# A hybrid decoder layer: bulk loads of the branch stage on ACT's queue, RG-LRU gate matmuls farther behind their split, one gate pair moved behind the RG-LRU pairs

## The chip, the cores and the metric

The kernel runs on one core of one Trainium2 chip. The metric is device microseconds of one execution. Engines are named as in the profile: PE is TensorE (PEld its weight loads), DVE is VectorE, ACT is ScalarE, POOL is GpSimd, SP is SyncE, which here does nothing but issue DMAs. "SPq", "ACTq" and "POOLq" are the instruction streams in which those engines issue DMAs. TensorE's granted clock is written as a share of 2.4 GHz; 0.5 would be its lower level, 1.2 GHz.

## The reference, cut to what matters

One layer of a decoder on 1104 tokens (16 meta, 1024 prompt, 8 x 8 decode), model width 1024. All arithmetic is float32 in the reference.

```
xn = rms_norm(x);  u, gate_a, q, f, i, og, m_a, m_b = split(xn @ w_in)     # eight blocks of 1024 columns
uc = causal_conv(u)
r, ig = sigmoid(block_diag(uc, rg_w)), sigmoid(block_diag(uc, ig_w))       # 8 blocks of 128 x 128
a = exp(-8 r softplus(-lam));  h = scan(a, sqrt(1 - a^2) * ig * uc)        # RG-LRU
y_a = h * gelu(gate_a)
y_b = rms_norm(hgrn2(q, f, i)) * silu(og)                                  # HGRN2
mixed = sigmoid(m_a) * (y_a @ w_branch_a) + sigmoid(m_b) * (y_b @ w_branch_b)
x = x + rms_norm(mixed @ w_out);  x = x + rms_norm(squared_relu_mlp(rms_norm(x)))
```

## The kernel before, in words

Every large matmul is done in float16 with three products (high x high, high x low, low x high), so weights and activations are split into a high half (ACT, a scaled copy) and a low half (DVE, the remainder); for weights this is `w_split`, lines 194 and 196. A *pair* is two 128-column blocks of a weight matrix against one activation matrix, computed for two halves of the tokens. Most pairs use a Strassen form: 7 products per half, each product 12 matmuls (lines 359, 361, 362 in `prod`), in the order S3, S1, A11, S2, A22, S4, A12 over four PSUM banks. Because A22 adds into the bank of S3, ACT has to copy that bank out (line 372) before the fifth product can start; bank by bank the same holds for the next ones. Pairs named in `NOSTR` use the plain form (`upair`): 8 products per half, and only 4 weight splits in place of 7.

Weights come in ahead of use, one pair ahead. SP loads a 512 KB `ws` tile (`raw_dma`, L164) and a 256 KB `sa` tile (`sum_load`, L182), later one more block (L239, or L261 in the plain form). For the Strassen form POOL adds further blocks onto these tiles with accumulating DMAs (L184, L233, L236, L242); the plain form has none of these four.

The stretch that matters runs from the pairs of `LSEQ` to the last branch pair:

1. **`LSEQ`**: eight RG-LRU pairs u0 to u7 (block h of `u` and of `gate_a`), and five gate pairs g3 to g7 (blocks of `m_a`, `m_b`, whose tanh goes to DRAM tensors `th_d[i]`, `th_store`, L1330). Behind each pair u*h* a generator `lru(h, ...)` does the RG-LRU of head h: convolution, the split of its result into `uh` (ACT, L1205) and `ul` (DVE, L1208), 18 gate matmuls of 376 columns (L1215 to L1217) with their tanh (L1218), the scan, the product with the gate, and stores of y to DRAM tensors `yb_d`.
2. **Preparation of the branches**, `y_prep`: for branch b, then for branch a, seven float16 operands are made from five 1.1 MB tensors of `yb_d`. Two generators (k = 0 and 2) each load 544 KB tiles `ys` (`load`, L1274), split them (L1280 on ACT, L1282 on DVE) and add them (L1287). Branch b's loads begin once the last RG-LRU has ended (`yb_start`, which also stores `out_o_conv` and `out_o_h`, and puts the new tiles in the room of the RG-LRU's); branch a's begin when branch b's operands are done (`ya_start`).
3. **Branch pairs** Yb0 to Yb3 (y_b @ w_branch_b) and Ya0 to Ya3 (y_a @ w_branch_a), columns in halves of 272. Yb pair p multiplies by the stored tanh, which `th_load(p)` (L1370) brings back from `th_d`, and `ac_store` (L1374) puts the result in DRAM, after which the next tanh tile, `th_load(p + 2)`, can go into one of the two `th` buffers. Ya pair p does the same with `th_load(p + 4)`, and `merge` adds the stored Yb result by accumulating DMAs (L1412). The last half of Ya3 uses an `ac` tile loaded on L1437.

The order on PE, DVE, ACT, POOL and SP is written out by hand there (`manual_schedule`): instructions stand in each engine's stream in the order of the Python code. The code is woven by a planner, `HQ`. Each generator yields triples (DVE cost, ACT cost, hold). After each product of a pair `hq.tick(rd, ra)` counts all holds down by one and adds rd and ra to two credits; a generator goes one step when its hold has run out and the credits it asks for are above zero. So a hold of n means "n products later". `ywait` forces steps out when a pair needs an operand that isn't split yet.

In `lru`, the low split `ul` is held 1 tick behind `uh`, and the first gate matmuls 2 ticks behind `ul`. In `y_prep` the first loads go out at once and the first split is held 5 ticks. All these loads, and those of `th_load` and `ac`, are `nc.sync.dma_start`: they stand in SP's stream between the loads of weights. A DMA whose tile isn't free yet holds up its stream until it is.

Of the kernel before, what the change touches and what calls it, by code (L numbers as in the profile page):

```python
# [60 lines left out]
        HPAIRS += [(FG + _h + 1, Q_ + _h + 1)]  # L61
GPAIRS = [(MB + 2 * i, MB + 2 * i + 1) for i in range(4)] + [(MA + 2 * i, MA + 2 * i + 1) for i in range(4)]
UPAIRS = [(U_ + h, G_ + h) for h in range(8)]
LSEQ = ["u0", "u1", "g3", "u2", "u3", "u4", "u5", "u6", "u7", "g4", "g5", "g6", "g7"]
NOSTR = ("u3", "u4", "u5", "u6", "u7")


@with_exitstack
def layer_kernel(ctx, tc, xT, w_pl, w_pr, w_o, w_up, w_dn, gw, par, sconv, slru, shg,
# [212 lines left out]
    class BG:  # L282
# [4 lines left out]
        def add(self, g):  # L287
            self.q.append(g)
# [897 lines left out]
    def lru(h, up, gm):  # L1186
# [16 lines left out]
        ul = lr.tile([P, CW], F16, tag="ul", name=nm("ul"))  # L1203
        ACT.activation(gwh, gws, AF.Copy, scale=SW)
        ACT.activation(uh, c1, AF.Copy, scale=SY)  # L1205
        yield 1.7, 0, 1
        DVE.scalar_tensor_tensor(gwl, gws, SW, gwh, op0=OP.mult, op1=OP.subtract)
        DVE.scalar_tensor_tensor(ul, c1, SY, uh, op0=OP.mult, op1=OP.subtract)  # L1208
        th = [lr.tile([P, CW], F32, tag=f"th{i}", name=nm("th")) for i in range(2)]
        for n, (a0, a1) in enumerate(CHU):  # L1210
            yield 0, 1.0, 1 if n else 2
            for i, bb in ((0, rbh), (1, ibh)):
                ps = bank("ht"[i])
                w = a1 - a0
                PE.matmul(ps[:, :w], gwh[:, i, :], uh[:, a0:a1], start=True, stop=False)  # L1215
                PE.matmul(ps[:, :w], gwh[:, i, :], ul[:, a0:a1], start=False, stop=False)
                PE.matmul(ps[:, :w], gwl[:, i, :], uh[:, a0:a1], start=False, stop=True)  # L1217
                ACT.activation(th[i][:, a0:a1], ps[:, :w], AF.Tanh, scale=0.5 / (SW * SY), bias=bb[:, h:h + 1])  # L1218
# [50 lines left out]
    def y_prep(s, scale, dst, pool, k, ready):  # L1269
        ks = slice(k, k + 2)  # L1270

        def load(n, tag):
            t = pool.tile([P, 2, HW], F32, tag=f"{tag}{k}", name=nm("ys"))
            nc.sync.dma_start(t, yb_d[s][n][:, ks])  # L1274
            return t

        def split(i, t, sc, hold=1):
            hi, lo = (x[:, ks] for x in dst(i))
            yield 0, 1.2, hold
            ACT.activation(hi, t, AF.Copy, scale=sc)  # L1280
            yield 1.3, 0, 1
            DVE.scalar_tensor_tensor(lo, t, sc, hi, op0=OP.mult, op1=OP.subtract)  # L1282
            ready.add((i, k))

        def add(t, x, hold):
            yield 1.3, 0, hold
            DVE.tensor_tensor(t, t, x, op=OP.add)  # L1287

        ta, tb = load(4, "yA"), load(3, "yB")
        yield from split(5, ta, scale, 5)  # L1290
        ta = load(0, "yA")
        yield from split(3, tb, scale)
        yield from split(0, ta, scale, 2)
        ta = load(2, "yA")
        yield from add(tb, ta, 5)
        yield from split(4, tb, scale)
        yield from split(2, ta, scale)
        ta = load(1, "yA")
        yield from add(tb, ta, 5)
        yield from split(6, tb, scale)  # L1300
        yield from split(1, ta, -scale)

# [64 lines left out]

    def th_load(i):
        ths[i] = gst.tile([P, 2, TO], F32, tag="th", name=nm("th"))
        nc.sync.dma_start(ths[i], th_d[i])  # L1370

    def ac_store(p):
        yield 0, 0, 2
        nc.gpsimd.dma_start(ac_d[p], ths[p])  # L1374
        th_load(p + 2)

    hq.drain([e[0] for e in hq.q if e[0] not in ygens[1]])
    th_load(0)
# [48 lines left out]
    def th_next(p, gs):  # L1427
        yield 0, 0, 1
        while hq.has(gs):
            yield 0, 0, 1  # L1430
        th_load(p)

    APLACES = ((0, 1, 2, 3, 5), (0, 2, 3, 5))
    ac = acp.tile([P, 2, TO], F32, name="ac")
    for p in range(4):
        if p == 2:
            nc.sync.dma_start(ac, ac_d[3])  # L1437
        ta = ths[p + 4]
        drain(cur["gen"])
        ops = cur["ops"]  # L1440
        gens = [prep(slot=iter([wo[2 * p + j]]))[1] for j in range(2)]
        begin()

        def chainw(gens=gens, last=cur["gen"]):
            for g in gens:
                yield from g
            yield from last

        cur["gen"] = chainw()
        mine = []  # L1450

        def done(m, c0, w, p=p, ta=ta, mine=mine):
            mine.append(hq.add(merge(2 * p + m, ta[:, m], ac_d[p][:, m], c0, w)))

        for c in range(2):
            def tk_(i):
                if i in APLACES[c]:
                    advance(cur["gen"], 1)
                hq.tick(0.8, 0.9)
                if i in APLACES[c]:  # L1460
                    advance(cur["gen"], 1)

            now = p == 3 and c == 1
            s0, s1 = (slab_branch(ta[:, m], merge_now(2 * p + m, ac[:, m]) if now else None) for m in range(2))
            if not now:
                def both(c0, w, x0, x1, s1=s1, f=s1.both):
                    f(c0, w, x0, x1)
                    done(1, c0, w)

                def one(e, c0, w, a, b=None, f=s0.one):  # L1470
                    f(e, c0, w, a, b)
                    if e == 0:
                        done(0, c0, w)

                s1.both, s0.one = both, one
            pair(ops, BYa, c * CQ, CQ, s0, s1, tk_)
        if p < 2:
            hq.add(th_next(p + 6, mine))
# [357 lines left out]
    with tc.manual_schedule(engines={E.PE, E.DVE, E.Pool, E.Activation, E.SP}):  # L1836
        late = lambda k: None
        for q in range(2, npair - 1):
            g, i = divmod(q, 8)
            ops = take()  # L1840
            for c in range(2):
                def split(k):
                    if k in PLACES[c]:
                        wadv(1)
# [160 lines left out]
```

## Time and profile before

| what | value |
|---|---|
| median of 3 runs | 1962.94 us (1962.11 to 1967.33) |
| profiled execution | 1960.88 us, of which the span is 1959.1 us |
| PE busy | 1795.1 us, 92% of the span |
| DVE busy | 1403.6 us, 72% |
| ACT busy | 1001.9 us, 51% |
| POOL busy | 452.8 us, 23% |
| mean granted TensorE clock | 0.972 |

How to read it: the span is the time from the first to the last instruction; the rest of the execution's own time lies around it. Busy shares are averages over stages with different limits, so a stretch is read by itself: how long PE stood idle in it, what ended each idle time, and at what clock PE ran. A matmul's own duration (0.28 us) overlaps its neighbours'; the distance between two starts is what it costs.

### The profile page before, as it was taken

Reading aid. Unit: us, or ns where it says so; the run is one execution under the profiler, and the core shown is the slowest. Engines: PE = TensorE matmul, PEld = TensorE weight load, DVE = VectorE, ACT = ScalarE, POOL = GpSimd, SP = SyncE. Lnnn points to the kernel's source line nnn. Section 1 sums busy time; section 2 is a strip of 40 time slices with the busy share of each in tenths; the row PEclk is TensorE's granted clock in tenths of the full one; section 3 lists DMA queues with packets and bytes.
Section 4 is the critical chain, followed back from the end, with each engine's and each line's share of the span. In section 5 each row is a group of like instructions: output and inputs, shape, how many; then the busy total and the mean of one; then the engine's idle time right before and its main releaser. Section 6 shows DMA issues by size and latency. Waiting matters only on the chain. (4 is left out here: it accounts for less than half of the span.)

```text
span 1959.1 us, 43578 instructions
## 1 busy us (share of the span) xinstructions
PE 1795.1 (92%) x17976; PEld 1532.5 (78%) x17976; DVE 1403.6 (72%) x2625; ACT 1001.9 (51%) x2115; POOL 452.8 (23%) x543
## 2 busy tenths in 40 slices
PE   5999999999999999897697879889999999999987
PEld 4888888888987777676576669877888888788777
DVE  7998889888855675756575556687547756756767
ACT  4555555555544656664442335456436526625653
POOL 3512211222222100111112324564111211111122
PEclk9899999999999999998899989899999999999999
DMA  5253332433355423356787863234454544454535
GB/s 176 64 110 87 90 95 70 127 83 97 94 145 127 113 89 78 81 129 199 232 245 206 214 149 88 59 78 102 112 107 102 113 109 100 105 116 101 137 77 161
DMA packets 123383, 233.43 MB, mean 119 GB/s; under 512 B 11696, under 2 KB 49456, under 8 KB 121520
## 3 DMA queue, kind: packets, MB, share of 16 engines
q0 software_dynamic: 47056, 95.93, 26.2%
q1 hardware_dynamic: 66880, 129.69, 20.2%
q10 hardware_dynamic: 9248, 5.02, 1.0%
q8 instruction: 140, 2.29, 0.5%
q14 instruction: 59, 0.48, 0.1%
HBM read 188.97 MB, written 41.63 MB: 118 GB/s over the span
## 5 line engine op out<-in xcount | busy, mean ns | idle before, releaser
L361 PEld LDWEIGHTS <-sh 128*128 128x128 f16 x3960 | 390.8, 99 | 147.0 <-issue 76.0
L362 PEld LDWEIGHTS <-sl 128*128 128x128 f16 x3960 | 390.9, 99 | 83.1 <-DVE sl L196 7.0
L359 PEld LDWEIGHTS <-sh 128*128 128x128 f16 x3960 | 391.5, 99 | 80.7 <-ACT sh L194 7.7
L359 PE MATMUL pd<-xh,sh 128*128 128x276 f16 (+1 forms) x976 | 277.3, 284 | 15.7 <-DVE et L459 11.8
L361 PE MATMUL pd<-xl,sh 128*128 128x276 f16 (+1 forms) x976 | 277.2, 284 | 0.0
L362 PE MATMUL pd<-xh,sl 128*128 128x276 f16 (+1 forms) x976 | 277.1, 284 | 0.0
L359 PE MATMUL q<-aoh,sh 128*128 128x272 f16 (+2 forms) x1008 | 259.6, 267 | 6.6 <-ACT sh L194 5.2
L362 PE MATMUL q<-aoh,sl 128*128 128x272 f16 (+2 forms) x1008 | 259.5, 267 | 3.4 <-DVE sl L196 3.4
L359 PE MATMUL q<-hoh,sh 128*128 128x272 f16 (+2 forms) x952 | 255.2, 273 | 7.4 <-DVE U L1744 3.4
L196 DVE SCALAR_TENSOR_TENSOR sl<-ws,sh 128x512 f16<-128x512 f32 x283 | 193.8, 687 | 94.5 <-ACT sh L194 94.0
L361 PE MATMUL q<-aol,sh 128*128 128x272 f16 (+2 forms) x1008 | 259.4, 267 | 0.0
L362 PE MATMUL q<-hoh,sl 128*128 128x272 f16 (+2 forms) x952 | 255.2, 273 | 1.0 <-DVE sl L196 1.0
L361 PE MATMUL q<-hol,sh 128*128 128x272 f16 (+2 forms) x952 | 255.2, 273 | 0.8 <-DVE hol L1513 0.8
L359 PE MATMUL pd<-tsh,sh 128*128 128x276 f16 (+1 forms) x800 | 227.4, 284 | 30.3 <-DVE U L376 13.7
L196 DVE SCALAR_TENSOR_TENSOR sl<-sa,sh 128x512 f16<-128x512 f32 x191 | 135.4, 710 | 149.0 <-ACT sh L194 147.7
L361 PE MATMUL pd<-tsl,sh 128*128 128x276 f16 (+1 forms) x800 | 227.5, 284 | 0.0
L362 PE MATMUL pd<-tsh,sl 128*128 128x276 f16 (+1 forms) x800 | 227.5, 284 | 0.0
L194 ACT ACTIVATE sh<-ws 128x512 f16<-128x512 f32 x283 | 169.8, 621 | 85.1 <-DMA ws<-in_w_pr 44.3
L194 ACT ACTIVATE sh<-sa 128x512 f16<-128x512 f32 x191 | 118.6, 623 | 133.5 <-DMA sa<-in_w_pr 72.9
L1009 PE MATMUL pd<-sh,xh 128*128 128x128 f16 (+1 forms) x576 | 103.4, 222 | 2.0 <-ACT F L478 2.0
L1011 PE MATMUL pd<-sh,xl 128*128 128x128 f16 (+1 forms) x576 | 103.5, 222 | 0.0
L1010 PE MATMUL pd<-sl,xh 128*128 128x128 f16 (+1 forms) x576 | 103.4, 222 | 0.0
(375 smaller groups left out, 4114.1 us busy)
## 6 DMA issues: line engine op xcount, KB each, us to landing
sa<-in_w_pr POOLq DMA_DIRECT2D x90, 256.0 KB, 4.2
ws<-in_w_pr SPq DMA_DIRECT2D x35, 512.0 KB, 4.0
sa<-in_w_up POOLq DMA_DIRECT2D x48, 256.0 KB, 3.8
sa<-in_w_dn POOLq DMA_DIRECT2D x48, 256.0 KB, 4.0
ys<-yb SPq DMA_DIRECT2D x20, 544.0 KB, 5.8
sa<-in_w_pr SPq DMA_DIRECT2D x35, 256.0 KB, 4.1
ws<-in_w_pr SPq DMA_DIRECT2D x35, 256.0 KB, 3.0
th<-th SPq DMA_DIRECT2D x8, 1088.0 KB, 5.7
```

Of the source, the lines that this page charges most:

```text
L194: ACT.activation(hi, src, AF.Copy, scale=SW)
L196: DVE.scalar_tensor_tensor(lo, src, SW, hi, op0=OP.mult, op1=OP.subtract)
L359: PE.matmul(o, h[:, k, :], bh[:, k, c0:c0 + w], start=first and k == 0, stop=False, skip_group_check=not first)
L361: PE.matmul(o, h[:, k, :], bl[:, k, c0:c0 + w], start=False, stop=False, skip_group_check=not first)
L362: PE.matmul(o, l[:, k, :], bh[:, k, c0:c0 + w], start=False, stop=(k == nk - 1), skip_group_check=not first)
L1009: PE.matmul(po, a, wh[:, k % 4, :], start=(k == 0), stop=False)
L1010: PE.matmul(po, a, wl[:, k % 4, :], start=False, stop=False)
L1011: PE.matmul(po, b, wh[:, k % 4, :], start=False, stop=(k == KT - 1))
```

## The change

`LSEQ` now runs u0 to u7 and then g3 to g7, and u2 takes the plain form. In `lru`, `ul` is held 2 ticks behind `uh` instead of 1, and the first gate matmuls 4 ticks behind `ul` instead of 2. The 20 loads of `y_prep`, the 8 of `th_load` and the one of `ac` are issued in ACT's stream. Their places move: `y_prep` starts its loads 1 (k = 0) and 3 (k = 2) ticks after it is added, with longer holds between load and use (8 for 5, 4 for 2, 6 for 5) and 2 ticks between the last reader of a tile and the next load into it; `ac_store` waits 6 ticks between the store and the next `th_load`, and leaves out the one for tile 5, which `th_late` does 7 ticks into Ya0; `th_next` waits 2 more ticks; `ac` is loaded one pair later.

```diff
-LSEQ = ["u0", "u1", "g3", "u2", "u3", "u4", "u5", "u6", "u7", "g4", "g5", "g6", "g7"]
-NOSTR = ("u3", "u4", "u5", "u6", "u7")
+LSEQ = ["u0", "u1", "u2", "u3", "u4", "u5", "u6", "u7", "g3", "g4", "g5", "g6", "g7"]
+NOSTR = ("u2", "u3", "u4", "u5", "u6", "u7")
...
         ACT.activation(uh, c1, AF.Copy, scale=SY)
-        yield 1.7, 0, 1
+        yield 1.7, 0, 2
...
         for n, (a0, a1) in enumerate(CHU):
-            yield 0, 1.0, 1 if n else 2
+            yield 0, 1.0, 1 if n else 4
...
             t = pool.tile([P, 2, HW], F32, tag=f"{tag}{k}", name=nm("ys"))
-            nc.sync.dma_start(t, yb_d[s][n][:, ks])
+            nc.scalar.dma_start(t, yb_d[s][n][:, ks])
...
+        yield 0, 0, 1 + k
         ta, tb = load(4, "yA"), load(3, "yB")
-        yield from split(5, ta, scale, 5)
+        yield from split(5, ta, scale, 8)
+        yield 0, 0, 2
         ta = load(0, "yA")
         yield from split(3, tb, scale)
-        yield from split(0, ta, scale, 2)
+        yield from split(0, ta, scale, 4)
+        yield 0, 0, 2
         ta = load(2, "yA")
-        yield from add(tb, ta, 5)
+        yield from add(tb, ta, 6)
         yield from split(4, tb, scale)
         yield from split(2, ta, scale)
+        yield 0, 0, 2
         ta = load(1, "yA")
-        yield from add(tb, ta, 5)
+        yield from add(tb, ta, 6)
...
     def th_load(i):
         ths[i] = gst.tile([P, 2, TO], F32, tag="th", name=nm("th"))
-        nc.sync.dma_start(ths[i], th_d[i])
+        nc.scalar.dma_start(ths[i], th_d[i])
 
     def ac_store(p):
         yield 0, 0, 2
         nc.gpsimd.dma_start(ac_d[p], ths[p])
-        th_load(p + 2)
+        if p < 3:
+            yield 0, 0, 6
+            th_load(p + 2)
...
     def th_next(p, gs):
         yield 0, 0, 1
         while hq.has(gs):
             yield 0, 0, 1
+        yield 0, 0, 2
+        th_load(p)
+
+    def th_late(p):
+        yield 0, 0, 7
         th_load(p)
...
     for p in range(4):
-        if p == 2:
-            nc.sync.dma_start(ac, ac_d[3])
+        if p == 0:
+            hq.add(th_late(5))
+        if p == 3:
+            nc.scalar.dma_start(ac, ac_d[3])
```

## Rows read from the trace of the kernel before

**Rows 1.** The page: PE's line, and its 40 slices of 49 us.
```profile
PE 1795.1 (92%) x17976; PEld 1532.5 (78%) x17976; DVE 1403.6 (72%) x2625; ACT 1001.9 (51%) x2115; POOL 452.8 (23%) x543
...
PE   5999999999999999897697879889999999999987
...
PEclk9899999999999999998899989899999999999999
DMA  5253332433355423356787863234454544454535
```

**Rows 2.** Windows: busy us (x instructions) of each engine, then PEclk, DMA share, GB/s.
```profile
600.00:895.00 295.00, 271.69 (x2162) 214.59 (x2160) 193.27 (x307) 180.88 (x337) 34.97 (x50) 0.97 0.40 100
895.00:946.00 51.00, 36.84 (x291) 29.36 (x289) 28.05 (x40) 21.81 (x36) 9.38 (x11) 0.90 0.82 230
946.00:1060.00 114.00, 96.71 (x768) 77.92 (x768) 78.81 (x127) 44.65 (x71) 16.80 (x21) 0.93 0.77 234
1060.00:1168.00 108.00, 77.41 (x602) 61.23 (x602) 62.31 (x115) 34.94 (x64) 31.17 (x30) 0.91 0.83 196
```

**Rows 3.** Waits of PE, 600 to 895 us: total, times, longest.
```profile
PE ph L1216 <- DVE ul L1208: 14.0, 7, 4.5
PE ph L1215 <- ACT uh L1205: 4.6, 4, 3.2
```

**Rows 4.** Windows of 20 us around the longest of these waits.
```profile
700.00:720.00 20.00, 15.91 (x106) 11.08 (x105) 10.09 (x16) 11.65 (x20) 2.90 (x3) 0.83 0.29 74
760.00:780.00 20.00, 16.83 (x121) 12.28 (x119) 11.15 (x16) 9.08 (x23) 1.94 (x4) 0.91 0.45 116
800.00:820.00 20.00, 20.00 (x152) 15.41 (x151) 7.94 (x13) 14.79 (x25) 1.72 (x2) 0.92 0.38 85
820.00:840.00 20.00, 15.49 (x102) 10.90 (x101) 13.77 (x23) 9.09 (x20) 2.59 (x3) 0.83 0.51 127
```

**Rows 5.** Timeline of PE: first matmuls of two adjoining products, 12 matmuls apart.
```profile
880.09 0.28 PE L359 MATMUL pd<-xh,sh 128*128 128x276 f16 x1
...
881.50 0.28 PE L359 MATMUL pd<-tsh,sh 128*128 128x276 f16 x1
```

**Rows 6.** Timeline of PE: matmuls behind the long gaps, idle time and releaser in brackets.
```profile
914.35 0.39 PE L359 MATMUL pd<-tsh,sh 128*128 128x276 f16 x1 [9.24 <-ACT U L372]
...
940.76 0.28 PE L359 MATMUL pd<-xh,sh 128*128 128x276 f16 x1 [2.66 <-DVE U L376]
...
946.16 0.28 PE L359 MATMUL pd<-ybh,sh 128*128 128x272 f16 x1 [2.42 <-DVE U L384]
...
975.47 0.39 PE L359 MATMUL pd<-ybh,sh 128*128 128x272 f16 x1 [7.80 <-DVE U L376]
...
1065.70 0.38 PE L359 MATMUL pd<-xh,sh 128*128 128x272 f16 x1 [6.43 <-DVE et L459]
```

**Rows 7.** Timeline of ACT: what it stood before in those gaps.
```profile
907.67 1.11 ACT L1280 ACTIVATE ybh<-ys 128x1088 f16<-128x1088 f32 x1 [7.76 <-DMA sa<-in_w_pr]
...
973.71 0.63 ACT L194 ACTIVATE sh<-sa 128x512 f16<-128x512 f32 x1 [11.17 <-DMA sa<-in_w_pr]
...
1063.95 1.15 ACT L194 ACTIVATE sh<-ws 128x512 f16<-128x512 f32 x2 [10.01 <-DMA ws<-in_w_pr]
```

**Rows 8.** Timeline of SP's stream: the issues ahead of those waits.
```profile
899.79 2.79 SPq L1274 DMA_DIRECT2D ys<-yb  x4
...
947.16 0.38 SPq L1370 DMA_DIRECT2D th<-th  x1
956.06 0.32 SPq L1370 DMA_DIRECT2D th<-th  x1
956.47 0.38 SPq L182 DMA_DIRECT2D sa<-in_w_pr  x1
...
1048.90 0.33 SPq L164 DMA_DIRECT2D ws<-in_w_o  x1
1057.46 0.33 SPq L1370 DMA_DIRECT2D th<-th  x1
1057.89 0.38 SPq L164 DMA_DIRECT2D ws<-in_w_pr  x1
```

**Rows 9.** Timeline of POOL: the last tanh store, and the addition onto the late `sa`.
```profile
949.54 0.71 POOL L1330 DMA_DIRECT2D th<-th  x1 [8.03 <-ACT U L372]
963.42 0.88 POOL L184 DMA_DIRECT2D sa<-in_w_pr  x1 [13.17 <-DMA sa<-in_w_pr]
```

**Rows 10.** Windows of 20 us around the gaps of rows 6.
```profile
900.00:920.00 20.00, 10.76 (x72) 7.93 (x70) 7.08 (x9) 6.35 (x9) 2.08 (x3) 0.74 0.99 288
...
960.00:980.00 20.00, 12.20 (x86) 9.37 (x86) 7.20 (x13) 6.47 (x10) 3.51 (x4) 0.76 0.78 208
...
1060.00:1080.00 20.00, 12.41 (x90) 9.60 (x90) 9.17 (x19) 4.56 (x9) 6.89 (x7) 0.83 0.88 217
```

**Rows 11.** Waits of SP's stream at the lines that move, 895 to 1168 us.
```profile
SPq L1370 <- DMA ac<-th: 36.7, 4, 11.1
...
SPq L1274 <- DVE ybl L1282: 16.5, 5, 7.3
...
SPq L1274 <- DVE xl L1282: 13.8, 2, 13.0
...
SPq L1274 <- DMA ys<-yb: 9.6, 3, 4.2
SPq L1370 <- DMA th<-th: 8.4, 1, 8.4
...
SPq L1274 <- DMA out_o_h<-hout: 3.8, 1, 3.8
```

## The prediction, made before the change was run

> **What bounds the kernel now.** I read the page first, then windows, then the waits of PE, and last the timelines of the engines that PE waits for. PE is busy 92% of the span, and its 40 slices show where it isn't: the thin digits stand in slices 16 to 25, and there alone the DMA line goes above 5 for long [rows 1]. So PE is the bound, and what can be won is its idle time there and the time that it runs below full clock. The windows cut this stretch in four [rows 2]: the RG-LRU pairs (600 to 895 us: 23.3 us idle, clock 0.97, DMA share 0.40), the last gate pairs (895 to 946: 14.2 us idle, clock 0.90), the Yb pairs (946 to 1060: 17.3 us, 0.93) and the Ya pairs (1060 to 1168: 30.6 us, 0.91). In the last three the DMA engines are 77 to 83% busy.
>
> Two causes must be told apart. In the first stretch PE waits for the split of the RG-LRU's own operand: 14.0 us for `ul` on DVE, 4.6 us for `uh` on ACT [rows 3]. In the others it waits for ACT or DVE, and these had waited for a DMA [rows 6, 7]: for `ys` loads (the 7.76 us before the first split; the four loads had gone out 8 us earlier) or for late weights. Why the weights are late stands in SP's stream [rows 8]: the second tanh load stood until 956.06 for the store of the last gate pair, which POOL had issued at 949.54 [rows 9], and the `sa` load behind it went out at 956.47. POOL could add to it at 963.42, ACT split it at 973.71, and PE stood 7.80 us [rows 6]. The same happens at 1057.46: a tanh load holds up a weight load, and PE stands 6.43 us.
>
> **The change, part by part.** A product is 12 matmuls and takes 1.41 us [rows 5], which is one tick of the planner.
>
> *Gate matmuls farther back.* `ul` gets two ticks more, 2.8 us, before PE wants it; `uh` three, 4.2 us. Of the seven waits for `ul` the longest was 4.5 us, so about 1.7 us of it remains; the others and the four for `uh` (longest 3.2) fit in, if DVE's backlog stays as it was. 18.6 us of waits shrink to 1.7. Behind these waits the clock is below full: 20 us at 0.83, 0.91, 0.92 and 0.83 [rows 4] are 3.4 + 1.8 + 1.6 + 3.4 = 10.2 us of full-speed work not done. I leave 1 us of it. Gain 16.9 + 9.2 = 26. From both sides: 10, if the backlog grows by what is given (each head's chain ends some three ticks later, and its scan then stands nearer to the next head's split), and 29, if all goes.
>
> *u2 in plain form.* Two halves by one more product of 1.41 us: 2.8 us lost on PE, which nothing hides. In return POOL's four additions and three weight splits fall away, on engines with room there (ACT 181 of 295 us [rows 2]): nothing. Part one is 26 - 2.8 = 23.
>
> *g3 behind u7.* Its 168 matmuls, POOL additions, SP loads and tanh store move with it, from a stretch with DMA share 0.40 into one with 0.82 [rows 2]. PE's work is the same. Worked through with the planner's holds and credits, 26 products stood between the end of the last RG-LRU and Yb0, and 36 do now. One generator of branch b's preparation has holds of 29 in sum before (6 + 2 + 3 for the first three splits, 5 + 4, 5 + 4), and 45 after (3 + 9 + 2 + 2 + 5, 2 + 6 + 4, 2 + 6 + 4, for k = 2). So its end still falls into Yb0. No price by itself; the room pays for the longer holds.
>
> *Loads on ACT, the first split 8 products behind its load.* 8 x 1.41 = 11.3 us for loads that took 7.9 us from issue (899.79) to the split (907.67) [rows 7, 8]: the 9.24 us gap goes, and with it the 5.2 us of clock (20 us at 0.74 [rows 10]). The gaps of 2.66 and 2.42 us behind it come from weights issued between `ys` loads; I count half of them. Gain 17. ACT's own wait for the `out_o_h` store (3.8 us on SP [rows 11]) lies inside the four products that PE can run before it needs ACT (5.6 us).
>
> *Tanh loads 0 and 1 on ACT.* They are not delayed, so the wait for the last tanh store moves to ACT: 949.54 to 956.06, 6.5 us [rows 8, 9]. PE runs 5.6 us of products and then stands until ACT has copied the first bank and done the splits queued behind it (two of 1.11 us and some weights [rows 7], my estimate 4 us): a new gap of about 5 us, plus 2 of clock. It replaces 7.80 us and 4.8 of clock (0.76 [rows 10]), since `sa` now goes out at once. Gain 5.6; none of the new gap would make it 12.6, twice of it -1.4.
>
> *Later tanh loads.* SP waited 36.7 us in 4 for the stores, 9.2 each [rows 11]. Three of these now have 6 ticks, 8.5 us, so ACT meets a rest of a few us, inside the cover of 5.6; the fourth (tile 5) goes 7 ticks into Ya0, and the 6.43 us gap goes with 3.4 of clock (0.83 [rows 10]). Gain 9.8. The Ya pairs' other gaps, which come from the accumulating DMAs of POOL, stay.
>
> *Issue cost.* 29 DMAs on ACT at 0.33 us, SP's price for one [rows 8], are 9.6 us, on an engine that is busy 101 of 273 us [rows 2]: hidden. Without cover it would be those 9.6.
>
> *Sum.* The three tail terms make 17 + 5.6 + 9.8 = 32. But the DMA engines were busy 0.82 x 51 + 0.77 x 114 + 0.83 x 108 = 219 us of these 273 [rows 2]; at a share of 0.9 the same transfers need 244, which leaves 29 to win, and as loads overlap more, each lands later. I take 20. Total 23 + 20 = 43 from the profiled execution's 1960.9, so 1918; the median stands 2 us above that execution, so **1920**. Bounds: 10 - 3 with nothing won in the tail, to 29 - 3 + 32, so 7 to 58 us.
>
> The Trainium skill, "DMA: Bandwidth & Descriptors", section "Issuing engines are not separate DMA queues", says that DMAs started by different engines run on the same 16 DMA engines and interleave, so that a second issuer only saves issue time. By that rule alone the tail's 20 us would not come, and the sum would be 1940. The trace shows something that the rule leaves aside: the load at 956.47 was late because its stream stood, not for want of an engine (share 0.78 in that window [rows 10]); that is why I keep the 20.
>
> **Rivals.**
>
> *The tail is bound by the DMA engines.* For it: 0.99 at 900 to 920 us, 0.88 at 1060 to 1080 [rows 10], and g3's transfers come on top. Against it: the waits above have an owner in SP's order. Then only part one counts: 1963 - 23 = 1940. It is what the rule of the skill named above would make of the time. Chance 0.20.
>
> *ACT stands where SP stood.* The waits at the moved lines sum to 89 us on SP [rows 11], where they cost PE only what weights were late. In ACT's stream the PSUM copies and all weight splits stand behind them. The place is Yb0 to Yb3: five tanh and ten `ys` loads whose tiles come free only as DVE gets there. It decides once ACT stands more than 5.6 us at one load, for then PE stands too. If two thirds of the 89 us reach PE, 59 go against the 43 + 2: 1963 - 45 + 59, about 1977. For it: the undelayed tanh load alone is 6.5 us. Against: 6 ticks and 2 ticks now stand before nearly all others. Chance 0.10.
>
> *Both parts bring little*, because the split's backlog grows and the tail is full: within 0.3%, or 6 us, which is about what a measurement of this kernel can tell from no change. Chance 0.04.
>
> *All gaps of the tail go too*, since each gap lengthens the next: three quarters of its 62 us idle [rows 2] are 46, and 1963 - 26 - 46 is about 1891. Chance 0.06.
>
> That the change does nothing can be left out: every hold changed is one that the planner obeys.
>
> **How the numbers follow.** The forecast has 0.60, with 1904 to 1940 as its own range. The range must leave out no more than 2 in 10: it takes in the DMA rival and its worse side (only 10 won in part one: 1952) and half of the best case: 1897 to 1952. Faster by over 0.3% are forecast, DMA rival and best case, 0.86; within it 0.04; slower 0.10.
>
> **What would show it.** Right: the waits of PE at L1215 and L1216 fall below 4 us in total, and the clock in the RG-LRU stretch is 0.99 or more; no L1274 or L1370 in SP's waits; the first `ys` split waits for no DMA; a gap of about 5 us in the first half of Yb0 behind an ACT that stands before a tanh load; no gap of 6 us in Ya0. Wrong: waits at L1216 of the old size; ACT standing over 5 us at several loads; weights as late as before with the DMA share above 0.9.

## The result and the profile after

The changed kernel takes **1946.20 us** (median of 4, 1935.49 to 1949.46) against 1965.13 us for the kernel before on the same chip: ratio **0.9893 [0.9849, 0.9936]**, so 1.1% faster. A second set of runs gave 1937.97 us and 0.9889 [0.9868, 0.9911]. The forecast was 1920, 43 us less; some 19 to 21 came. The profiled execution took 1946.51 us, 14.4 less than that of before.

The page of the changed kernel: PE's totals and the 40 slices, now of 48.6 us.

```profile
PE 1792.0 (92%) x18000; PEld 1532.9 (79%) x18000; DVE 1397.6 (72%) x2615; ACT 998.4 (51%) x2115; POOL 448.2 (23%) x539
...
PE   5899999999999999988697869889999999999987
...
PEclk9999999999999999999799989999999999999999
DMA  5253333433444233477688853225544544454635
```

Against [rows 1], PE's line (slices counted from 0) is full up to slice 16, where it was up to 15, and the thin part that is left has two slices at 6, where it had one. In the clock's line slice 19 (924 to 972 us) shows 7, where none was below 8: the new notch. The DMA line is as full there as before. The windows say how much each stage won. The first runs from the start of the RG-LRU pairs to g3, the next three start at g3, at the first matmul of Yb0 and at that of Ya0; the last two lie inside Yb0.

```profile
606.00:800.80 194.80, 192.48 (x1593) 155.60 (x1591) 140.19 (x216) 130.65 (x250) 14.91 (x31) 1.00 0.34 87
800.80:923.00 122.20, 106.96 (x873) 85.81 (x871) 74.23 (x121) 67.28 (x122) 22.25 (x26) 0.99 0.68 182
923.00:1031.90 108.90, 85.24 (x673) 68.04 (x673) 71.60 (x113) 40.39 (x66) 16.17 (x20) 0.87 0.77 228
1031.90:1145.00 113.10, 86.39 (x675) 68.39 (x673) 65.93 (x119) 37.56 (x67) 31.78 (x31) 0.92 0.84 201
920.00:940.00 20.00, 7.72 (x65) 6.14 (x63) 7.49 (x13) 5.87 (x12) 1.80 (x3) 0.81 0.85 248
940.00:960.00 20.00, 12.61 (x55) 7.68 (x55) 11.26 (x15) 5.64 (x7) 1.48 (x2) 0.51 0.33 84
```

The RG-LRU stretch runs without a hole: 2.3 us idle at clock 1.00, where [rows 2] had 23.3 us at 0.97. That window of [rows 2] ran on into the gate pairs; up to the first of them, and then up to and through the Yb pairs, the kernel before shows this:

```profile
600.00:841.40 241.40, 223.10 (x1761) 175.39 (x1759) 155.63 (x245) 145.12 (x272) 27.09 (x41) 0.96 0.38 96
841.40:946.16 104.76, 85.43 (x692) 68.55 (x690) 65.85 (x103) 57.56 (x101) 17.26 (x21) 0.95 0.65 172
946.16:1045.95 99.79, 85.16 (x672) 68.55 (x672) 71.22 (x113) 40.29 (x64) 16.24 (x20) 0.91 0.80 241
```

So the RG-LRU stretch was idle for 18.3 us there. The Yb pairs are worse than before: 23.7 us idle at 0.87, for 14.6 at 0.91. The same in the waits, of PE and of ACT:

```profile
PE ph L1216 <- DVE ul L1208: 2.3, 5, 0.8
...
PE pd L359 <- ACT U L372: 4.4, 1, 4.4
...
ACT U L372 <- DMA th<-th: 11.3, 1, 11.3
...
ACT U L372 <- DMA out_o_h<-hout: 7.2, 1, 7.2
```

Of the 18.6 us in [rows 3] 2.3 are left. In their place stand two waits of ACT for a DMA, which ACT did not have before: they were SP's [rows 8, 11]. PE's timeline shows what they cost (idle time and releaser in brackets), with two of the gaps in the Ya pairs behind them:

```profile
870.38 0.28 PE L359 MATMUL pd<-tsh,sh 128*128 128x276 f16 x1 [4.39 <-ACT U L372]
...
941.87 0.38 PE L359 MATMUL pd<-ybh,sh 128*128 128x272 f16 x1 [13.10 <-ACT ybh L1280]
...
1057.87 0.39 PE L359 MATMUL pd<-tsh,sh 128*128 128x272 f16 x1 [5.32 <-DVE U L376]
...
1084.07 0.39 PE L359 MATMUL pd<-tsh,sh 128*128 128x272 f16 x1 [4.57 <-DVE U L376]
```

And the timelines of the other engines around the first three:

```profile
869.04 0.84 ACTq L1274 DMA_DIRECT2D ys<-yb  x2
869.92 0.40 ACT L372 ACTIVATE U<-pd 128x276 f32<-128x276 f32 x1 [7.19 <-DMA out_o_h<-hout]
...
926.19 11.61 ACTq L1374 DMA_DIRECT2D th<-th  x2
937.84 0.40 ACT L372 ACTIVATE U<-pd 128x272 f32<-128x272 f32 x1 [11.30 <-DMA th<-th]
...
938.27 0.44 DVE L376 TENSOR_TENSOR U<-U,pd 128x272 f32<-128x272 f32 x1 [11.89 <-ACT U L372]
...
939.40 1.28 DVE L1287 TENSOR_TENSOR ys<-ys,ys 128x1088 f32<-128x1088 f32 x1
...
926.83 0.70 POOL L1334 DMA_DIRECT2D th<-th  x1 [7.14 <-ACT th L518]
...
1041.45 1.13 SPq L182 DMA_DIRECT2D sa<-in_w_pr  x1
...
1047.42 0.86 POOL L184 DMA_DIRECT2D sa<-in_w_pr  x1 [8.82 <-DMA sa<-in_w_pr]
1047.96 1.20 POOL L233 DMA_DIRECT2D sa<-in_w_pr  x1
1048.50 1.55 POOL L236 DMA_DIRECT2D ws<-in_w_pr  x1
```

(`th_load` is L1374 and `th_store` L1334 now.) At 926.19 ACT comes to the two tanh loads (one line, x2). The second wants the room of the last gate pair's tile, whose store POOL issues at 926.83; ACT copies the next bank only at 937.84. DVE stands 11.89 us for that copy, and behind it in DVE's stream is the addition (L1287) that makes the next operand of branch b, which ACT then splits (L1280): PE goes on at 941.87. The third gap is of another kind: POOL's additions for the current pair (L233, L236) stand behind one for the next pair (L184), which waits for a load that SP had issued 6 us earlier.

### The profile page after: what moved, and what is told of

The parts are those of the page before. It is cut to its first block, busy times and chain, and to the rows that moved or that the text cites. A ratio compares the mean times of both kernels' runs of the same rounds, so it can differ in the third digit from the quotient of the medians.

```text
span 1944.7 us, 43580 instructions
## 1 busy us (share of the span) xinstructions
PE 1792.0 (92%) x18000; PEld 1532.9 (79%) x18000; DVE 1397.6 (72%) x2615; ACT 998.4 (51%) x2115; POOL 448.2 (23%) x539
## 3 DMA queue, kind: packets, MB, share of 16 engines
q1 hardware_dynamic: 62704, 108.52, 17.2%
## 5 line engine op out<-in xcount | busy, mean ns | idle before, releaser
L359 PE MATMUL pd<-xh,sh 128*128 128x276 f16 (+1 forms) x1016 | 285.6, 281 | 12.7 <-DVE et L459 5.0
L361 PE MATMUL pd<-xl,sh 128*128 128x276 f16 (+1 forms) x1016 | 285.5, 281 | 0.0
L362 PE MATMUL pd<-xh,sl 128*128 128x276 f16 (+1 forms) x1016 | 285.3, 281 | 0.0
L359 PE MATMUL pd<-tsh,sh 128*128 128x276 f16 (+1 forms) x768 | 218.9, 285 | 30.6 <-DVE U L376 16.7
L362 PE MATMUL pd<-tsh,sl 128*128 128x276 f16 (+1 forms) x768 | 219.3, 286 | 0.0
L361 PE MATMUL pd<-tsl,sh 128*128 128x276 f16 (+1 forms) x768 | 219.1, 285 | 0.0
```

What stands on the lines that cost most here:

```text
L359: PE.matmul(o, h[:, k, :], bh[:, k, c0:c0 + w], start=first and k == 0, stop=False, skip_group_check=not first)
L361: PE.matmul(o, h[:, k, :], bl[:, k, c0:c0 + w], start=False, stop=False, skip_group_check=not first)
L362: PE.matmul(o, l[:, k, :], bh[:, k, c0:c0 + w], start=False, stop=(k == nk - 1), skip_group_check=not first)
```

## The experiments

All of them in one table, in us of each kernel's profiled execution: u0 to Yb0, the Yb pairs, and from Ya0 to the end of the span. (The first column starts with u0's second product in every row. The code in front of it is the same in all but e8, e10 and e11, whose edit acts in the whole kernel. This start lies at 598.8 to 606.1 us, the latest in the profile of the changed kernel, so some 5 us of that profile are not the change's.) The stages come from one execution each; those of e5, e7 and e10 were 2 to 8 us longer than the median of their kernel. The last column holds, behind the four Ya pairs, some 800 us of `w_out` and the MLP, and these alone vary from 795.1 to 801.0 us; so the Ya pairs by themselves are named in the text where they matter. The ratio is that to the kernel before, run on the same chip beside it.

| kernel | u0 to Yb0 | Yb | Ya0 to end | ratio [95%] |
|---|---|---|---|---|
| before | 344.8 | 99.8 | 913.2 | |
| changed | 316.9 | 108.9 | 912.8 | 0.9893 [0.9849, 0.9936] |
| changed, again (e0) | 316.8 | 106.3 | 909.1 | 0.9889 [0.9868, 0.9911] |
| e1: changed, tanh load 1 later | 316.5 | 99.3 | 912.5 | 0.9858 [0.9843, 0.9873] |
| e2: changed, loads on SP | 313.0 | 98.4 | 914.0 | 0.9836 [0.9819, 0.9853] |
| e3: before, RG-LRU holds alone | 316.5 | 108.3 | 914.5 | 0.9908 [0.9884, 0.9932] |
| e4: e1, branch b's loads later | 318.3 | 103.4 | 910.8 | 0.9870 [0.9846, 0.9893] |
| e5: before, queue alone | 337.7 | 116.1 | 913.8 | 1.0033 [1.0019, 1.0048] |
| e6: e2, tanh load 1 later | 312.8 | 94.1 | 914.5 | 0.9807 [0.9783, 0.9830] |
| e7: e2 in the old order | 304.4 | 133.7 | 913.2 | 0.9960 [0.9943, 0.9976] |
| e8: e6, POOL's order | 307.0 | 90.2 | 903.4 | 0.9709 [0.9689, 0.9729] |
| e9: e6, old holds of `y_prep` | 324.5 | 98.3 | 912.3 | 0.9865 [0.9845, 0.9885] |
| e10: before, POOL's order alone | 337.0 | 99.2 | 909.8 | 0.9917 [0.9889, 0.9946] |
| e11: e1, POOL's order | 308.8 | 93.5 | 897.9 | 0.9747 [0.9707, 0.9786] |

### Which part of the change does what: e3, e5, e2

**e3** takes the kernel before and changes two holds:

```diff
-        yield 1.7, 0, 1
+        yield 1.7, 0, 2
...
-            yield 0, 1.0, 1 if n else 2
+            yield 0, 1.0, 1 if n else 4
```

> The kernel before with only the two longer holds in the RG-LRU (low split 2, gate matmuls 4). Theory (these holds are worth the 26 us that PE stood and ran below full clock at L1215 and L1216, and need nothing else of the change): waits at L1216 below 4 us in total, 1936 to 1942. Rival (the order of the pairs and the plain u2 are what makes room for them): waits at L1216 above 8 us, 1952 to 1962.

Measured: 1940.14 us against 1959.65, so 0.92% of the change's 1.1% come from two numbers. PE's waits at L1216 are what the theory asked for:

```profile
PE ph L1216 <- DVE ul L1208: 1.6, 3, 0.8
```

u0 to Yb0 gets 28.3 us shorter. But 8.5 of these are given back in the Yb pairs: PE comes to Yb0 sooner, the operands of branch b do not, and splits are forced out inside Yb0 (gaps of 2.95 and 2.63 us, released by ACT's L1280).

**e5** takes the kernel before and changes the queue of the 29 loads, **e2** the changed kernel and puts them back. The edit is the same, on three lines:

```diff
-            nc.sync.dma_start(t, yb_d[s][n][:, ks])
+            nc.scalar.dma_start(t, yb_d[s][n][:, ks])
...
-        nc.sync.dma_start(ths[i], th_d[i])
+        nc.scalar.dma_start(ths[i], th_d[i])
...
-            nc.sync.dma_start(ac, ac_d[3])
+            nc.scalar.dma_start(ac, ac_d[3])
```

> The kernel before with only the queue changed: the 29 loads in ACT's stream at their old places, with the old holds. Theory (a wait costs more in ACT's stream than in SP's, where PE's slack is four products): ACT stands at more than three loads for over 5 us each, 1985 to 2015. Rival (ACT has room, and the weights gain what ACT loses): 1955 to 1968.

> The changed kernel with all 29 moved loads back in SP's stream; order, holds and plain u2 as changed. Theory (a load that waits holds up the stream that it stands in, ACT's or SP's): no stand of ACT at a load, but SP stands 7 to 11 us at tanh load 1 and 5 to 8 us at the first load of branch b, the weights behind them come late and PE has a gap of 5 to 9 us each time; 1938 to 1950, about the changed kernel's time. Rival (only the bandwidth counts, the queue is of no matter): Yb0 keeps its gap of 13 us and half clock, within 3 us of 1946. Rival (SP's stands were the whole loss of the tail, as the prediction had it): 1955 or more.

Measured: **the queue alone makes the kernel before 0.33% slower** (1967.21), and **the changed kernel is faster without it** (1928.09 us; 0.9836 against 0.9889 in the changed kernel's second set, and the intervals do not overlap). e5's Yb pairs take 116.1 us for 99.8. The timeline of ACT in e5, around two of the loads:

```profile
951.99 0.33 ACTq L1370 DMA_DIRECT2D th<-th  x1
952.36 0.40 ACT L372 ACTIVATE U<-pd 128x272 f32<-128x272 f32 x1 [9.44 <-issue]
...
987.24 0.33 ACTq L1370 DMA_DIRECT2D th<-th  x1
987.61 0.40 ACT L380 ACTIVATE U<-pd 128x272 f32<-128x272 f32 x1 [7.17 <-DMA ac<-th]
```

ACT stands 9.44 and 7.17 us, and the copy of a PSUM bank comes 0.37 us behind each load ("issue" in the brackets only says that the view names no other releaser). ACT stands for 7 to 10 us right behind such a load at five places. That is the mechanism of the prediction's rival "ACT stands where SP stood", in the places that it named. Its price was far too high (59 us there, and a theory of 1985 us and more here): the Yb pairs lose 16.3 us, and the stretch in front of them wins 7.1. So the time fell into the range of the milder rival (1955 to 1968), which said that the weights gain about what ACT loses.

In e2 it is SP that stands, as the timeline of its stream shows:

```profile
917.17 10.25 SPq L1374 DMA_DIRECT2D th<-th  x2
927.51 0.38 SPq L182 DMA_DIRECT2D sa<-in_w_pr  x1
```

The wait is about the same (SP stands 9.5 us, ACT 11.3), but what stands behind it is a weight load, and PE's gap for it is 2.85 us in place of 13.10:

```profile
946.34 0.28 PE L359 MATMUL pd<-ybh,sh 128*128 128x272 f16 x1 [2.85 <-DVE U L376]
```

All three expectations for e2 were too slow (1938 us and more): the theory named this wait, and took PE's gap behind it as 5 to 9 us. The Trainium skill, "DMA: Bandwidth & Descriptors", section "Issuing engines are not separate DMA queues", says that another issuer saves only the time of issuing. The trace agrees: in both kernels the move saved nothing. What it cost is what ACT had to do behind its loads.

### The 13 us gap: e0, e1, e6

**e0** is the changed kernel again, in five rounds.

> The changed kernel again, beside the kernels that differ from it by one thing. Theory (its stands of ACT at the out_o_h store and at tanh tile 1 repeat): ratio 0.987 to 0.992 to the kernel before, a stand of ACT over 8 us at tanh tile 1, Yb0's clock again below 0.9. Rival (its first profile caught a rare bad landing): ratio 0.982 to 0.986, like the variant with SP's queue.

Measured: ratio 0.9889 [0.9868, 0.9911]; gaps of 4.55 and 14.46 us at the same two places. They belong to the order, not to one execution.

**e1** is the changed kernel with the second tanh load eight products into Yb0, **e6** the same edit on e2:

```diff
     th_load(0)
-    th_load(1)
+
+    def th_one():
+        yield 0, 0, 8
+        th_load(1)
+
+    hq.add(th_one())
```

> The changed kernel, with the load of tanh tile 1 issued 8 ticks into Yb0 instead of ahead of it. Theory (ACT's stand of 11.3 us before that load made the gap of 13.1 us and the half clock behind it): ACT waits for no DMA of a tanh tile, the 37 us from Yb0's start in which PE was idle 18.6 us and the clock 0.63 shrink by 20 to 28 us, and the time is 1918 to 1928 us, a ratio of 0.976 to 0.981 to the kernel before. Rival 1 (the gap is branch b's last split, forced in Yb0 before its load has landed): a gap of 6 to 10 us stays in Yb0 behind the operand split, 1934 to 1942. Rival 2 (the DMA engines bound the tail): what is won in Yb0 comes back by Ya0, 1940 to 1948.

> The changed kernel with all moved loads in SP's stream, and tanh tile 1 issued 8 ticks into Yb0. Theory (SP's stand of 9.5 us at that tile makes the next sa load late and with it the gap of 2.9 us in Yb0): no such stand, sa goes out some 8 us sooner, Yb 3 to 6 us shorter, 1922 to 1926. Rival (the sa load is not what ends that gap; the forced splits are): Yb within 1.5 us, 1926 to 1930.

Measured: 1931.09 and 1922.29 us. In e1 ACT's wait for `th<-th` is gone, and the Yb pairs take 99.3 us for 108.9 (106.3 in e0). So the early issue of that one load costs some 7 to 10 us there; by the ratios (0.9858 for e0's 0.9889, whose intervals just touch) it is about 6 in the whole. Not all of the 13 us come back, and the time lies between the ranges of e1's theory and its rivals: the splits of branch b are still forced out in Yb0, and now show as gaps of their own, of which 1.95 us at 926.27 (ACT's L1280) and 2.70 at 937.98 (DVE's `ybl`) are the longest. In e6, where SP stood, the Yb pairs win 4.3 us. With this edit the queue is worth the same as without: 0.9858 on ACT, 0.9807 on SP.

### The wait for `out_o_h`: e4

**e4** adds to e1 that branch b's first loads go out five products later:

```diff
-        yield 0, 0, 1 + k
+        yield 0, 0, (6 if s else 1) + k
...
-        yield from split(5, ta, scale, 8)
+        yield from split(5, ta, scale, 4 if s else 8)
```

> The changed kernel with tanh tile 1 issued 8 ticks into Yb0 and branch b's first loads 6 ticks (k = 0) and 8 ticks (k = 2) behind the end of the RG-LRU instead of 1 and 3, the first split held 4 instead of 8. Theory (ACT's other stand, 7.2 us before the first load, made the gap of 4.4 us and what follows it): no wait of ACT for out_o_h, the stretch from the first late gate pair to Yb0 shrinks from 122 to 114 to 118 us, 1922 to 1928, 4 to 8 us under the variant with tanh tile 1 alone. Rival (branch b's preparation ends later by these ticks and is forced out in Yb0): Yb longer by 4 to 8 us and no gain, 1929 to 1935.

Measured: 1935.11 us, no faster than e1 (0.9870 against 0.9858, within the intervals). The gap of 4.4 us at the first load is gone, but the preparation ends later, and the splits forced out in Yb0 cost gaps of 3.38 and 4.90 us. The wait was moved, not won: the rival was right.

### What the order and the longer holds do: e7, e9

**e7** is e2 with `LSEQ` and `NOSTR` of the kernel before, **e9** is e6 with the holds of `y_prep` of the kernel before:

```diff
-LSEQ = ["u0", "u1", "u2", "u3", "u4", "u5", "u6", "u7", "g3", "g4", "g5", "g6", "g7"]
-NOSTR = ("u2", "u3", "u4", "u5", "u6", "u7")
+LSEQ = ["u0", "u1", "g3", "u2", "u3", "u4", "u5", "u6", "u7", "g4", "g5", "g6", "g7"]
+NOSTR = ("u3", "u4", "u5", "u6", "u7")
```

```diff
-        yield 0, 0, 1 + k
         ta, tb = load(4, "yA"), load(3, "yB")
-        yield from split(5, ta, scale, 8)
-        yield 0, 0, 2
+        yield from split(5, ta, scale, 5)
         ta = load(0, "yA")
...
-        yield from split(0, ta, scale, 4)
-        yield 0, 0, 2
+        yield from split(0, ta, scale, 2)
...
-        yield from add(tb, ta, 6)
+        yield from add(tb, ta, 5)
...
-        yield 0, 0, 2
         ta = load(1, "yA")
-        yield from add(tb, ta, 6)
+        yield from add(tb, ta, 5)
```

> All holds as changed, all moved loads in SP's stream, but the pairs in the old order (g3 behind u1, u2 in Strassen form). Theory (the fifth gate pair behind the RG-LRU gives branch b's preparation room; without it more of it is forced out in Yb0): the sum of the stretches from u0 to w_out grows by 5 to 12 us, Yb by most of it, 1933 to 1940. Rival (the order is worth nothing, the plain u2 costs 2.8 us): 1923 to 1928.

> The kernel of the run with SP's queue and tanh tile 1 late, with the preparation of the branches as before the change (loads at once, holds 5, 2, 5, 5, no steps between last reader and next load). Theory (the longer holds let branch b's last splits end in Yb0, where they cost gaps of 7 us; with the old holds the preparation ends before Yb0, but SP stands at the loads and weights come late): the gaps behind the operand splits in Yb0 fall below 3 us, waits of ACT for weights from the late gates to Yb0 grow by 5 us or more, 1919 to 1928. Rival (the longer holds are worth what they were made for): 1930 to 1940. Rival (they only cost): 1910 to 1917.

Measured: e7 1952.22 us, 24 slower than e2, twice the most that its theory gave; e9 1936.44, as its first rival had it, and by the ratios (0.9865 for 0.9807) some 11 slower than e6. Without g3 behind u7 the longer holds don't fit: PE is at Yb0 after 304.4 us, and the Yb pairs take 133.7. PE's timeline in e7, behind Yb0's start:

```profile
928.61 0.38 PE L359 MATMUL pd<-ybh,sh 128*128 128x272 f16 x1 [10.78 <-ACT ybh L1280]
...
940.32 0.39 PE L359 MATMUL pd<-ybh,sh 128*128 128x272 f16 x1 [9.10 <-ACT ybh L1280]
...
949.04 0.38 PE L359 MATMUL pd<-ybh,sh 128*128 128x272 f16 x1 [6.10 <-ACT ybh L1280]
```

So the longer holds of `y_prep` need the moved pair: e7, which has them without it, is slower than e3, which has neither (0.9960 for 0.9908). It is not so the other way: e9, with the moved pair and the old holds, is at 0.9865. What e2 wins beside the two RG-LRU holds (0.9836 for 0.9908 in e3) comes from the moved pair, the longer holds, the plain u2 and the later tanh loads together; no run has the moved pair, the plain u2 or the later tanh loads alone, so their shares stay open.

### The Ya pairs: e8, e10, e11

The forecast's 9.8 us in the Ya pairs did not come in any of these kernels: Ya0 to the end is 909 to 915 us in all up to here. Up to the first matmul of `w_out`, the four pairs took 116.3 us before, 113.1 in the changed kernel and 111.6 in e0; the others lie at 112 to 118. The third gap of the result's timelines points at a reason: POOL's stream. **e8** takes e6 and issues the addition onto the next pair's tile (L184) behind the current pair's (L233, L236), in the whole kernel:

```diff
             if kind == "pr":
-                nc.gpsimd.dma_start(q, src[:, 1], accum_op=OP.add)
+                pend.append((q, src))
             sums.append((q, src))
+
+    pend = []
+
+    def sum_acc():
+        while pend:
+            q, src = pend.pop(0)
+            nc.gpsimd.dma_start(q, src[:, 1], accum_op=OP.add)
...
             yield from sp("A11", b)
             nc.gpsimd.dma_start(b, src[:, 0], accum_op=OP.add)
+            sum_acc()
             yield
```

(`sum_acc` also follows the two calls of `sum_load` that stand outside this sequence.) **e10** is this edit on the kernel before, **e11** the same on e1, so that e11 differs from e8 in the queue alone.

> The kernel of the run with SP's queue and tanh tile 1 late, with one more edit, in the whole kernel: the addition onto the next pair's sa tile stands behind the two additions that the current pair waits for, not ahead of them. Theory (in the Ya pairs POOL stands 8 to 9 us before that addition, because the tile's load has only just gone out, and the urgent additions stand behind it in POOL's stream; this, not SP's stand at tanh tile 5, ends the gaps of Ya): the gaps of 4 us and more in Ya fall below 2, Ya shrinks from 113 to 100 to 107 us, and the time is 1905 to 1916. Rival (the additions themselves are slow, the DMA engines being 81% busy there): Ya within 3 us, 1919 to 1925.

> The kernel before, with POOL's addition for the next pair moved behind the additions of the current one, and nothing else. Theory (POOL's order is a wait of its own, that the change neither made nor removed): the part from Ya0 to the end gets some 10 us shorter than the 913 us of before, and the pairs in front of it a few us; ratio 0.988 to 0.994. Rival (the order costs something only where loads come as close together as in the kernel with the new holds; in the kernel before SP's stands before tanh loads make the weights late anyway): ratio 0.997 to 1.002, and Ya0 to the end stays within 3 us of 913.

> The changed kernel (its loads on ACT's queue) with the second tanh load eight products later and with POOL's addition moved behind; it differs from the best kernel so far, 0.9709, in the queue alone. Theory (the queue costs what it cost with the old order of POOL, 0.9858 against 0.9807): ratio 0.974 to 0.978. Rival (with the weights in time, ACT's stands no longer meet a late split, or SP's stands no longer matter): ratio 0.968 to 0.972, no difference from the one with SP's queue.

Measured: **e8 takes 1904.93 us (1899.76 to 1909.91), ratio 0.9709, and beats both kernels.** In the profiles 21 us lie between it and e6, 5.8, 3.9 and 11.1 in the three stages; the Ya pairs take 102.8 us for 113.5. The gaps left in Ya are longer than the theory asked (up to 3.59 us, not below 2). POOL's waits in this stretch (total, times, longest), first of e6, then of e8, where L192 is the old L184 and L241 the old L233:

```profile
POOL sa L184 <- DMA sa<-in_w_pr: 59.6, 5, 15.6
```

```profile
POOL sa L241 <- DMA sa<-in_w_pr: 11.9, 3, 8.7
...
POOL sa L192 <- DMA sa<-in_w_pr: 5.3, 3, 4.1
```

59.6 us in which POOL stood for a load have become 17.2, most of it now at an addition for the current pair. The windows of e8's Yb and Ya pairs:

```profile
907.40:997.60 90.20, 82.78 (x674) 67.36 (x673) 72.09 (x113) 40.84 (x65) 16.16 (x20) 0.94 0.90 273
997.60:1100.50 102.90, 88.45 (x675) 69.68 (x673) 62.47 (x114) 36.04 (x64) 31.54 (x31) 0.90 0.89 213
```

The DMA engines are busy 0.90 and 0.89 here, against 0.77 and 0.84 in the changed kernel: they had room, so they were not what bound the changed kernel's tail.

e10 has the ratio that the theory gave (0.9917), but in another place, as far as its profile shows (it was the slowest of five executions, 1949.45 us for a median of 1941.81): 7.8 us of it lie before Yb0, and only 3.4 in the part from Ya0, where 10 were expected; those 3.4 are within the spread of the kernels above, and the Ya pairs alone are 4.3 us shorter. There the rival came nearer. In e10's Ya0 the tanh load on SP still makes a weight late, as the streams of SP, ACT and PE show:

```profile
1046.29 0.33 SPq L1380 DMA_DIRECT2D th<-th  x1
1046.71 0.44 SPq L164 DMA_DIRECT2D ws<-in_w_pr  x1
...
1054.49 1.15 ACT L201 ACTIVATE sh<-ws 128x512 f16<-128x512 f32 x2 [11.15 <-DMA ws<-in_w_pr]
...
1056.25 0.39 PE L369 MATMUL pd<-xh,sh 128*128 128x272 f16 x1 [7.08 <-DVE et L469]
```

ACT waits 11.15 us for that weight, and PE 7.08 us, as it waited 6.43 in [rows 6]. So the Ya pairs have **two owners of one delay**: SP's stand before the tanh load, and POOL's addition for the next pair. The change takes away the first alone, and the Ya pairs get 3.2 us shorter (4.7 in e0); e10 takes away the second alone, 4.3 us; e8 and e11 take away both, 13.5 and 15.2 us. Or, with POOL's edit by itself: it is worth 4.3 us in the kernel before, but 10.7 on e6 and 11.9 on e1.

e11 gave 1906.48 us and 0.9747 [0.9707, 0.9786]. That agrees with the theory's range, but the interval reaches e8's (0.9709 [0.9689, 0.9729], on another chip run): whether the queue still costs something, once POOL's order is mended, stays open.

## Why the prediction was wrong, point by point

Worked out for the profiled executions, with g3's 14 products at 1.41 us [rows 5] taken as 19.7 us: the forecast had 23 us in the RG-LRU pairs, 17 in front of Yb0, 5.6 in Yb and 9.8 in Ya, 55 in all, capped to 43. It came to **25.5, 2.3, -9.1 and 0.4**, less the 4.7 us of a later u0, which make the 14.4. (The 0.4 are 3.2 us won in the Ya pairs and 2.9 lost behind them, where nothing was changed.) The measured time lies inside the stated range; what fell short is the tail.

**"Gate matmuls farther back" and "u2 in plain form" were right** in their sum; the price of the plain u2 was not tried alone. Before, the RG-LRU stretch took 240.0 us (601.4 to 841.4) with g3 in it, so 220.3 without; it takes 194.8. Forecast 23, measured 25.5, of which 1.9 are only moved: as the gate matmuls stand farther back, 30 of them lie behind g3's start, where 18 lay behind g4's, at 0.16 us each. So it is 23.6, and e3 shows the holds alone, with 28.3 us for 26. The waits at L1215 and L1216 fell to 2.3 us where "below 4" was asked, and the clock is 1.00 where 0.99 was asked. The lower bound, a backlog of DVE that grows by as much as is given, did not show.

**"g3 behind u7" was right** in that the longer holds stand on it (e7), and took no price of its own that the windows show beside its 14 products. That the room would be enough was too kind: splits are still forced out in Yb0 in e1.

**"Loads on ACT, the first split 8 products behind its load"** was the first step that failed. The 9.24 us gap did go, and no split of `ys` waits for a DMA. But of the 17 us only some 2 came. "ACT's own wait for the `out_o_h` store (3.8 us on SP) lies inside the four products that PE can run" had both numbers wrong: ACT waited 7.2 us, not 3.8, and was covered for 3.3 (ACT idle from 862.7, PE from 866.0), not 5.6. That made the gap of 4.39 us. From the first late gate pair to Yb0, PE's idle time fell only from 19.3 to 15.2 us (with one pair more): the small waits stayed, 10.1 us in sum before, beside the 9.24, and 10.9 after, beside the 4.39, where half of two of them (2.66 and 2.42) had been counted as won. The 5.2 us of clock did not come at all: above what its matmuls take at full clock PE was busy for some 3.5 us in both. And 1.9 us of gate matmuls moved in. Which edit keeps the small waits was not tried alone; that e8 comes to Yb0 5.8 us sooner than e6 puts a part of them on POOL's order.

**The clock terms of the tail were twice what the matmuls lost.** For 900 to 920 us the sum has 9.24 us of gap and 5.2 of clock. But the 72 matmuls of that window are six products, 8.5 us at 1.41 [rows 5]; so all that was lost in it is 11.5 us, and 2.3 of these to the clock. The share of 0.74 is a mean over the window, the gap included, and so part of the gap was counted twice. In the same way the 4.8 and 3.4 us of the other two windows [rows 10] are 2.2 and 2.0: their 86 and 90 matmuls were busy for 12.20 and 12.41 us, and take 0.116 us each at full clock (925.83 to 927.11 for eleven of them in the changed kernel). Together 6.5 us were lost where 13.4 were put in, so some 7 of the tail's 32 us were never there. In the windows of [rows 4], whose waits are short, the two ways of counting agree to some tenths of a us.

**"Tanh loads 0 and 1 on ACT" is the step that failed most**: +5.6 forecast, 9.1 lost, all of it idle time (PE is busy 85.2 us in the Yb pairs of both kernels). Mechanism and place were as forecast, the size was not. The gap was worked out as wait less cover plus what ACT does behind it, 6.5 - 5.6 + 4 = 5. Measured: 11.3 - 2.2 + 4.0 = 13.1 us. The last term was right (937.84 to 941.87). The wait was taken from one store of before, and that was the quickest of the four late tanh stores of that kernel (us from issue to landing):

```profile
DMA to landing us min/median/max: 6.4/8.9/14.2
```

In the changed kernel the same store took 10.6 us, and 11.9 in e0. And the cover was not four products: what PE needed next was not only a free bank but an operand, `ybh`, whose addition on DVE and split on ACT both stood behind the load; PE ran on for 2.2 us (926.5 to 928.8). The clock was put at 2 us. By the matmuls it cost 6.2: the 55 of 940 to 960 us take 6.4 us at full clock and were busy for 12.61. Over all Yb pairs a low clock cost as much as in the kernel before, as the equal busy times show.

**"Later tanh loads"**: the 6.43 us gap went, as forecast, but of the 9.8 us 3.2 came in the Ya pairs (4.7 in e0). What was late next was not named: POOL's additions, in a stream that the prediction had set aside ("the Ya pairs' other gaps, which come from the accumulating DMAs of POOL, stay"). They did not only stay, they took the room that the other had left; e8, e10 and e11 show the pair.

**The rivals.** "ACT stands where SP stood" came true at two loads out of 29, which cost the change less than the RG-LRU holds won (e3), so the whole is still faster; by e2 the queue cost 0.5%. It had been set up as a case by itself, all or nothing, when a part of it stood in the forecast's own sum: the undelayed tanh load. "The tail is bound by the DMA engines" gave 1940, near what came, but by luck: e8 excludes its reason.

## What to carry to other kernels

A DMA that may have to wait belongs into the stream whose next work can stand longest: behind SP's it is a transfer that is late, behind ACT's it is every copy and split. Cover is counted from what the bound engine needs next, an operand as much as a free bank, at that place and not from the engine's usual slack. A wait is priced from all stores or loads of its kind in the trace, not from one, and a clock that is a mean over a window with a gap in it counts part of that gap again. And where two streams both make a transfer late, taking one away shows little: ask which row would be next, and take both away in one kernel before the first is called worthless.

## What the runs showed of the hardware that was not expected

A tanh store of 1.1 MB took from 6.4 to 14.2 us from issue to landing within the kernel before, and the last one, for which a load waits, took 6.4 there and 10.6 and 11.9 in two profiles of the changed kernel. The wait for `out_o_h` was 3.8 us on SP before and 7.2 on ACT after; a wait also depends on when its stream comes to it. The DMA share was 0.85 in the 20 us around the slow tanh store. What sets these times was not tried.

After the 13.10 us gap the granted clock of the window from 940 to 960 us was 0.51, about the lower level of 1.2 GHz, and its 55 matmuls took 6.2 us more than at full clock, about half of the gap's length once more. After the gap of 9.24 us in the kernel before it was 2.3 us up to the end of the window of [rows 10].
